# Turning the state-space values by VectorE and DRAM instead of TensorE, in a two-layer hybrid decoder on one core

## The chip, the core and the metric

One core of a Trainium2 chip runs the whole program in one launch. The metric is the device time of a launch in microseconds (us). Engines are named as in the profile: PE is TensorE's matmul row, PEld its weight load, DVE is VectorE, ACT is ScalarE, POOL is GpSimd, SP is the engine that issues most DMAs; a q behind a name (SPq, POOLq) is the engine's sequencer. L285 is line 285 of the kernel before.

## The reference

Two layers work on a sequence of 512 positions of width 1024, in float32. Each layer is

```python
hn = rmsnorm(x, pre_g)
proj = hn @ w_in                      # 1024 -> 6664, split into thirteen parts
y = concat([retention(q, k, v) * silu(g),            # 4 heads of 128, chunks of 128
            ssd_mixer(xbc, z, dt, ...),              # 8 heads of 64, 2 groups, state 128
            stick_breaking(q, k, v) * silu(g),       # 4 heads of 128
            memory_read(q, mem_n, w_mem_kv) * silu(g)])  # 4 heads of 128, 256 memory tokens
x = x + rmsnorm(y @ w_out, post_g)
```

The part that the change touches is the state-space mixer (`ssd_mixer`). In it a convolution and a SiLU give `xs` (values), `bm` and `cm`; then

```python
xdt = x_heads * delta[..., None]                     # values times step size
y_diag = einsum('bclsgj,bcsgjp->bclgjp', cb[..., None] * decay_in, xdt)
states = einsum('bclgn,bclgjp->bcgjpn', bc, xdt * decay_states[..., None])
y = rmsnorm_by_group((y_diag + y_off + x_heads * d_skip) * silu(z))
```

## The kernel before, in words

Activations lie features first: a tile of 128 features by 512 positions. Projections run as three fp32r products (high by high, high by low, low by high) of a split weight and a split activation; that is `mm3`, and nearly all of TensorE's time.

**Weights.** Both layers' weights come in 78 blocks of up to 1 MB, two subs of 128 x 1024 to a block, 156 subs in all (`k` = 0 to 155; 78 to a layer). `w_prefetch` splits a sub: ScalarE copies it to the high part, VectorE subtracts for the low part (`split`, L293 and L294). Five subs have a buffer (`NSUB = 5`), so sub `k` can be split when `k - 5` has been used. In the first half of the output projection and in the per-head projections a sub lasts 24 matmuls of 512 columns; in the second half of the output projection the four banks run two steps apart (`SKEW = 2`), so four subs are in use at once.

**Order.** `tick()` counts units, one to a projection of 128 columns (two to some others). `defer(n, f)` writes the work of `f` into the program `n` units later. A planner then fixes each engine's instruction order from the program order and its own estimate of what is ready; `keep_in_program_order` pins an instruction behind everything already written for its engine. Every engine runs its list strictly in order, and so does the SP queue that issues nearly all small DMAs.

**State-space group** (`ssd_group`, twice a layer). Units: the two value tiles `X["x"]`, a stick-breaking gate, B, C, a gate, two z gates. `ssd_values`, two units after the values, turns the two tiles of 128 features by 512 positions on TensorE (eight transposes of 128 x 128 into PSUM, L1003), multiplies by `delta` into `xdt` (L1007) and by the decay into `xds` (L1009). `ssd_mix`, `ssd_states` and `ssd_out` follow with their matmuls, then `ssd_var` (sum of squares, a one-row product, the row through ScalarE, DRAM and GpSimd to a broadcast) and `ssd_norm` (L1075), whose results the output projection uses as its last four inputs (`kc` 12 to 15).

**Turning through DRAM** (`columns_turned`) exists already for B and for retention's keys: VectorE transposes 32 x 32 blocks (L660), four DMAs per tile write the blocks to their places in DRAM (L663), and a read brings the turned tile back (L668).

**Retention** (`ret_head`, ..., `ret_head3`). `ret_head3` makes the one-row product of two heads and sends it the same way (ScalarE L808, SP L811, GpSimd L812 and L813, SP L815 and L818); `scaled` (L886) multiplies it in, seven units later.

**Tile pools**: 33 tiles "s", 16 "y", 9 "r" of 128 x 512; PSUM four banks "pj" (projections) and four "mx".

Of the kernel before, what the change touches and what calls it, by code (L numbers as in the profile page):

```python
# [8 lines left out]
F32 = mybir.dt.float32  # L9
# [3 lines left out]
ALU = mybir.AluOpType  # L13
# [3 lines left out]
P = 128  # L17
# [52 lines left out]
NBLK = len(BLOCKS)  # L70
# [4 lines left out]
def block_width(b):  # L75
    return 2 * (SUBD if BLOCKS[b % NBLK][0] == "d" else SUBW)
# [77 lines left out]

BLK = 32
TT = "y"
ST, SL, SB1, SB2 = "s", "y", 2, 4
ROW = 128  # L160

# [9 lines left out]
def v3(ap, a):  # L171
    return ap.rearrange("p (a b) -> p a b", a=a)


class Builder:
# [136 lines left out]
    def w_prefetch(self, upto=None, between=()):  # L312
        if self.starting and upto is None:
            return
        while self.w_split < (upto or min(self.nsubs, self.w_cur + self.NSUB)):
            k = self.w_split
            self.w_load(k // 2)
            n = block_width(k // 2) // 2
            h, l = (self.wp.tile([P, SUBW], F32R, tag=t, name=self.name(t), bufs=self.NSUB)[:, :n] for t in ("wh", "wl"))
            r = self.raw[k // 2]  # L320
            if isinstance(r, list):
                pieces = [(r[2 * (k % 2) + i][:], slice(512 * i, 512 * i + 512)) for i in range(2)]
            else:
                cs = [slice(0, n)] if k > 1 else [slice(0, n // 2), slice(n // 2, n)]
                pieces = [(r[:, (k % 2) * n + c.start:(k % 2) * n + c.stop], c) for c in cs]
            for i, (x, c) in enumerate(pieces):
                self.split(x, h[:, c], l[:, c], h[:, c].bitcast(F32))
                if i < len(between):
                    between[i]()
            self.sub[k] = (h, l)  # L330
            self.w_split += 1
            if k % 2:
                del self.raw[k // 2]
                if not self.starting:
                    self.w_load(k // 2 + self.NRAW)

    def w_load(self, b):
        while self.w_dma <= min(b, DEPTH * NBLK - 1):
            n = block_width(self.w_dma)
            src = self.a["wts"][self.w_off:self.w_off + P * n].rearrange("(p n) -> p n", p=P)  # L340
            if self.starting and self.w_dma == 2:
                r = [self.new(512, F32, "y") for _ in range(4)]
                for i in range(4):
                    self.nc.sync.dma_start(r[i][:], src[:, 512 * i:512 * i + 512])
            else:
                r = self.wp.tile([P, 2 * SUBW], F32, tag="raw", name=self.name("raw"), bufs=self.NRAW)
                if self.starting:
                    for c in ((slice(0, n),) if self.w_dma > 1 else (slice(0, n // 2), slice(n // 2, n))):
                        self.nc.sync.dma_start(r[:, c], src[:, c])  # L349
                        if not self.w_dma and not c.start:  # L350
                            self.mem_start()
                else:
                    self.nc.scalar.dma_start(r[:, :n], src)
            self.raw[self.w_dma] = r
            self.w_dma += 1
            self.w_off += P * n
# [273 lines left out]
    def mem_turn(self, h, w, y):  # L630
        nc = self.nc
        pT = []
        for m in range(2):
            T = self.buf(tag="y")
            for i in range(2):
                x = w[i].rearrange("p (t m j b) -> p m t j b", t=2, m=2, b=BLK)[:, m]
                nc.vector.transpose(T.rearrange("p (j t b) -> p t j b", t=NT, b=BLK)[:, 2 * i:2 * i + 2], x)
            d = self.turned_rows(P, SEQ)
            dd = d.rearrange("(j m) (a t) -> a m j t", m=BLK, a=P // BLK)
            pT.append(self.through_dram(T, dd, d, self.buf(tag="y")))  # L640
# [5 lines left out]
    def through_dram(self, T, dst, src, out):  # L646

        n = dst.shape[2]
        for a in range(P // BLK):
            self.nc.sync.dma_start(dst[a], v3(T[BLK * a:BLK * a + BLK], n))  # L650
        self.nc.sync.dma_start(out, src)
        return out

    def columns_turned(self, tiles, out):
# [3 lines left out]
        for k, x in enumerate(tiles):  # L658
            T = self.buf(n, TT)
            self.nc.vector.transpose(T, x)  # L660
            dd = d[:, P * k:P * k + P].rearrange("(b t) (a f) -> a t b f", t=BLK, a=P // BLK)
            for a in range(P // BLK):
# [188 lines left out]
    def ret_head2(self, h, v, sc, f, st, q, y):  # L851

        nc = self.nc
        b, o = self.mx(), slice(HD * h, HD * h + HD)
        for i in range(2):
            c = slice(2 * P * i, 2 * P * i + 2 * P)
            p = v[2 * i][0]
            self.mm3(b[:, c], p.h[:, o], p.l[:, o], sc.h[:, c], sc.l[:, c], True, False)
            if i:
                self.mm3(b[:, c], st[:, :P], st[:, P:], q.h[:, c], q.l[:, c], False, False)  # L860
            self.mm(b[:, 2 * P * i + P:2 * P * i + 2 * P], v[2 * i + 1][1][:, o], f[:, P * i:P * i + P], False, True)
        nc.scalar.copy(y, b)
        sq = self.buf(tag="r")
        nc.scalar.activation(sq, b, AF.Square, scale=HD ** -0.5)
        for n in (64, 32):
            nc.vector.tensor_add(sq[0:n], sq[0:n], sq[n:2 * n])
        if h % 2 == 0:
            self.z = self.new(512, F32R, "r"), []
        z, ys = self.z
        r = 64 * (h % 2)  # L870
        nc.scalar.copy(z[r:r + 32], sq[0:32])
        nc.vector.tensor_sub(z[r + 32:r + 64], sq[0:32], z[r:r + 32].bitcast(F32))
        ys.append(y)
        if h % 2:
            self.defer(3, self.ret_head3, h // 2, z, ys)

    def ret_head3(self, i, z, ys):

# [80 lines left out]
    def ssd_group(self, l, g, ysb):  # L959

        X = {"l": l, "g": g}
        self.ssd_decay(X)
        X["x"] = [self.conv(self.proj_b(), 2 * g + i) for i in range(2)]
        self.defer(2, self.ssd_values, X)
        self.gated(("sb", 2 * g), ysb[2 * g])
        X["b"] = self.conv(self.proj_b(), 4 + g)
        X["bt"] = self.buf()[:, :3 * P]
        self.columns_turned([X["b"][:, :3 * P]], [X["bt"]])
        X["c"] = self.conv(self.proj_b(), 6 + g)
        self.defer(3, self.ssd_mix, X)  # L970
        self.gated(("sb", 2 * g + 1), ysb[2 * g + 1])
        X["y"] = [self.buf(tag="y"), self.buf(tag="y")]
        X["z"] = [self.gate(self.proj_b()) for _ in range(2)]
        self.defer(1, self.ssd_states, X)
        self.defer(3, self.ssd_out, X, 0)
        self.defer(3, self.ssd_out, X, 1)
        self.defer(5, self.ssd_var, X)
        self.defer(9, self.ssd_norm, X)

    def ssd_decay(self, X):  # L980
        nc, S = self.nc, self.ssd
# [12 lines left out]
    def ssd_values(self, X):  # L994

        nc, g = self.nc, X["g"]
        X["xdt"], X["xds"] = [], []
        for i in range(2):
            b = self.mx()
            for c in (2 * i, 2 * i + 1):  # L1000
                for j in range(2):
                    o = 256 * (c % 2) + P * j
                    nc.tensor.transpose(b[:, o:o + P], X["x"][j][:, P * c:P * c + P], self.con("ident", P))  # L1003
            xdt, xds = self.buf(), self.buf()
            for c in (2 * i, 2 * i + 1):
                s = slice(256 * (c % 2), 256 * (c % 2) + 256)
                nc.vector.tensor_tensor(out=v3(xdt[:, s], 4), in0=v3(b[:, s], 4), in1=self.per_head("delta", g, c), op=ALU.mult)  # L1007
                if c < NT - 1:
                    nc.vector.tensor_tensor(out=v3(xds[:, s], 4), in0=v3(xdt[:, s], 4), in1=self.per_head("dst", g, c), op=ALU.mult)  # L1009
            X["xdt"].append(xdt)  # L1010
            X["xds"].append(xds)
# [323 lines left out]
```

## Time and profile before

| | |
|---|---|
| runs | 922.54, 922.68, 923.47 us; median 922.68 |
| the profiled execution | 923.25 us, of it 921.5 us from the first to the last instruction |
| busy: PE / DVE / ACT / POOL | 913.2 / 673.3 / 443.5 / 146.3 us |
| instructions: PE / DVE / ACT / POOL | 4667 / 1081 / 841 / 208 |
| DMA | 128.53 MB; mean 139 GB/s over the span |

Matmuls overlap in a pipeline, so what a matmul costs is the distance from its start to the next start and not its own duration; the view of the chain that ended last gives those distances, summed over stretches.

### The profile page before, as it was taken

The numbers are of one execution on the slowest core, as the hardware profiler recorded it, in microseconds if no ns is written. First come the engines' busy times: TensorE is split into PE (matmuls) and PEld (weight loads), VectorE is DVE, ScalarE is ACT, GpSimd is POOL, SyncE is SP. The second block draws the span as 40 slices with busy tenths as digits, with TensorE's granted clock in tenths as the row PEclk, the third lists the DMA queues.
The fourth block names the chain that finished last, engine by engine and source line by source line (L and its number), as shares of the span: only waits on it lengthen the run. The fifth ranks groups of instructions, "written<-read, shape, count | busy, mean of one in ns | idle before, by whom it ended". The sixth has DMA issues, their size and how long they took to land.

```text
span 921.5 us, 12952 instructions
## 1 busy us (share of the span) xinstructions
PE 913.2 (99%) x4667; PEld 773.6 (84%) x4667; DVE 673.3 (73%) x1081; ACT 443.5 (48%) x841; POOL 146.3 (16%) x208
## 2 busy tenths in 40 slices
PE   9999999999999999999999999999999999999997
PEld 7998888888888888888899888888888888888885
DVE  6855689888787887844587476898778869687343
ACT  6643485744453342733465336675445434335341
POOL 1200152320131110100040002423112120102001
PEclk9999999999999999999999999999999999999999
DMA  8544664642444333444345256556333362422502
GB/s 316 213 141 144 169 167 104 199 146 61 120 134 148 116 109 126 137 149 158 116 173 196 93 172 183 124 122 183 103 109 116 110 194 92 139 95 88 210 12 91
DMA packets 105408, 128.53 MB, mean 139 GB/s; under 512 B 64640, under 2 KB 79744, under 8 KB 96256
## 3 DMA queue, kind: packets, MB, share of 16 engines
q10 hardware_dynamic: 10224, 73.44, 23.4%
q1 hardware_dynamic: 95120, 54.28, 20.7%
q8 instruction: 36, 0.59, 0.3%
q14 instruction: 28, 0.23, 0.1%
HBM read 112.10 MB, written 15.56 MB: 139 GB/s over the span
## 4 chain that ended last, share of the span: by engine, by line
PE 98%; DMA 1%; ACT 0%; DVEq 0%; SPq 0%; POOLq 0%; issue 0%; POOL 0%; ACTq 0%; DVE 0%
PE pj L285 74%; PE mx L285 23%; PE mx L479 1%; DMA mem<-memT 1%; PE mx L1003 0%; ACT s L523 0%; DVEq L1331 0%; ACT s L1168 0%; POOLq L1331 0%; ACT wh L293 0%; SPq L506 0%; SPq L349 0%; SPq L1206 0%; POOL t L449 0%; ACTq L1331 0%
## 5 line engine op out<-in xcount | busy, mean ns | idle before, releaser
L285 PE MATMUL pj<-hTh,wh 128*128 128x512 f32 x704 | 276.4, 393 | 0.0
L285 PE MATMUL pj<-hTh,wl 128*128 128x512 f32 x704 | 275.8, 392 | 0.0
L285 PE MATMUL pj<-hTl,wh 128*128 128x512 f32 x704 | 274.6, 390 | 0.0
L294 DVE TENSOR_TENSOR wl<-raw,wh 128x1024 fp32r<-128x1024 f32 (+2 forms) x156 | 188.6, 1214 | 116.9 <-ACT wh L293 115.7
L293 ACT CAST wh<-raw 128x1024 fp32r<-128x1024 f32 (+2 forms) x156 | 158.7, 1020 | 205.0 <-PE pj L285 177.5
L285 PEld LDWEIGHTS pj<-hTh,wl 128*128 128x128 f32 x704 | 132.2, 188 | 27.3
L285 PEld LDWEIGHTS pj<-hTh,wh 128*128 128x128 f32 x704 | 132.3, 188 | 27.1 <-DVE s L593 0.8
L285 PEld LDWEIGHTS pj<-hTl,wh 128*128 128x128 f32 x704 | 132.3, 188 | 26.6
L285 PE MATMUL pj<-wh,s 128*128 128x512 f32 x320 | 97.6, 391 | 0.0
L285 PE MATMUL mx<-s,s 128*128 128x256 f32 (+4 forms) x528 | 79.7, 307 | 0.0
L285 PE MATMUL mx<-wh,s 128*128 128x512 f32 x256 | 79.2, 389 | 0.0
L285 PEld LDWEIGHTS mx<-s,s 128*128 128x128 f32 (+1 forms) x528 | 65.8, 177 | 8.2 <-PE pj L285 1.4
L285 PEld LDWEIGHTS pj<-wh,s 128*128 128x128 f32 x320 | 59.7, 188 | 12.4
L285 PE MATMUL pj<-wl,s 128*128 128x512 f32 x160 | 60.2, 389 | 0.0
L285 PEld LDWEIGHTS mx<-wh,s 128*128 128x128 f32 x256 | 48.1, 188 | 10.0
L294 DVE TENSOR_TENSOR s<-y,s 128x512 fp32r<-128x512 f32 x64 | 41.2, 687 | 19.7 <-ACT s L293 14.0
L262 ACT ACTIVATE s<-s 128x128 f32<-128x128 f32 (+3 forms) x96 | 41.8, 478 | 22.3 <-DVE s L733 20.6
L675 POOL TENSOR_TENSOR s<-y,s 128x512 fp32r<-128x512 f32 x16 | 23.7, 1494 | 179.9 <-ACT s L674 179.4
L293 ACT CAST s<-y 128x512 fp32r<-128x512 f32 x64 | 36.6, 617 | 30.8 <-PE mx L285 22.0
L285 PE MATMUL mx<-wl,s 128*128 128x512 f32 x128 | 49.6, 389 | 0.0
L285 PE MATMUL pj<-wl,hTh 128*128 128x256 f32 (+2 forms) x144 | 47.6, 331 | 0.0
L285 PE MATMUL pj<-wh,hTl 128*128 128x256 f32 (+2 forms) x144 | 47.5, 330 | 0.0
(185 smaller groups left out, 1298.5 us busy)
## 6 DMA issues: line engine op xcount, KB each, us to landing
raw<-wts ACTq DMA_DIRECT2D x69, 1024.0 KB, 4.8
s<-x SPq DMA_DIRECT2D x24, 256.0 KB, 4.1
y<-turned SPq DMA_DIRECT2D x24, 256.0 KB, 2.8
turned<-y SPq DMA_DIRECT2D x64, 64.0 KB, 2.2
s<-acs SPq DMA_DIRECT2D x16, 256.0 KB, 6.3
r<-row SPq DMA_DIRECT2D x12, 256.0 KB, 5.0
raw<-wts SPq DMA_DIRECT2D x4, 512.0 KB, 7.5
raw<-wts SPq DMA_DIRECT2D x2, 1024.0 KB, 6.3
```

Of the source, the lines that this page charges most:

```text
L262: i = self.nc.scalar.activation(out, in_, func, **k)
L285: return self.nc.tensor.matmul(out, lhsT, rhs, start=start, stop=stop)
L293: self.nc.scalar.copy(h, src)
L294: self.nc.vector.tensor_sub(l, src, hf)
L479: x = self.nc.tensor.transpose(b[:, P * j:P * j + P], hn[i][:, P * j:P * j + P], self.con("ident", P))
L675: nc.gpsimd.tensor_sub(p.l, x, p.hf)
```

## The change

1. The value tiles are turned by `columns_turned` right after their convolution, into two "r" tiles; the 32 TensorE transposes (8 to a group, 2 groups, 2 layers) are gone. `xdt` is written over the turned tile. `ssd_values` comes four units after the values instead of two, and the first multiplication by `delta` of each tile is pinned in program order.
2. `ret_head3` comes five units after its second head instead of three.
3. `ssd_var` and `ssd_norm` come two units later (7 and 11 for 5 and 9).
4. The low part of every third sub (`k % 3 == 2`, from 14 on, without those with `k % 78` from 16 to 33) is subtracted by GpSimd instead of VectorE: 36 of 156 subs.

```diff
+VD, HOLD = 4, True
 BLK = 32
-TT = "y"
+TT, TX = "y", "r"
...
-                self.split(x, h[:, c], l[:, c], h[:, c].bitcast(F32))
+                nc = self.nc
+                nc.scalar.copy(h[:, c], x)
+                (nc.gpsimd if self.low_by_pool(k) else nc.vector).tensor_sub(l[:, c], x, h[:, c].bitcast(F32))
...
+    def low_by_pool(self, k):
+
+        return k > 12 and k % 3 == 2 and not 16 <= k % (2 * NBLK) < 34
...
-            self.defer(3, self.ret_head3, h // 2, z, ys)
+            self.defer(5, self.ret_head3, h // 2, z, ys)
...
-        self.defer(2, self.ssd_values, X)
+        X["xt"] = [self.buf(tag=TX), self.buf(tag=TX)]
+        self.columns_turned(X["x"], X["xt"])
+        self.defer(VD, self.ssd_values, X)
...
-        self.defer(5, self.ssd_var, X)
-        self.defer(9, self.ssd_norm, X)
+        self.defer(7, self.ssd_var, X)
+        self.defer(11, self.ssd_norm, X)
...
-            b = self.mx()
-            for c in (2 * i, 2 * i + 1):
-                for j in range(2):
-                    o = 256 * (c % 2) + P * j
-                    nc.tensor.transpose(b[:, o:o + P], X["x"][j][:, P * c:P * c + P], self.con("ident", P))
-            xdt, xds = self.buf(), self.buf()
+            b = xdt = X["xt"][i]
+            xds = self.buf()
             for c in (2 * i, 2 * i + 1):
                 s = slice(256 * (c % 2), 256 * (c % 2) + 256)
-                nc.vector.tensor_tensor(out=v3(xdt[:, s], 4), in0=v3(b[:, s], 4), in1=self.per_head("delta", g, c), op=ALU.mult)
+                k = nc.vector.tensor_tensor(out=v3(xdt[:, s], 4), in0=v3(b[:, s], 4), in1=self.per_head("delta", g, c), op=ALU.mult)
+                if HOLD and not c % 2:
+                    self.tc.keep_in_program_order(k)
```

## Rows read from the trace of the kernel before

**Rows 1.** The head of the page: the span, the busy time of each engine (share of the span, instructions), and the granted TensorE clock in 40 equal slices (9 is 90% or more).

```profile
span 921.5 us, 12952 instructions
PE 913.2 (99%) x4667; PEld 773.6 (84%) x4667; DVE 673.3 (73%) x1081; ACT 443.5 (48%) x841; POOL 146.3 (16%) x208
PEclk9999999999999999999999999999999999999999
```

**Rows 2.** All waits of the PE in the whole span: who waited for whom, us in total, times, the longest.

```profile
PE mx L285 <- POOL b L197: 1.2, 1, 1.2
PE pj L285 <- ACT s L523: 1.0, 2, 0.7
```

**Rows 3.** The transposes' own line: count, duration in ns (minimum, median, maximum), first and last start.

```profile
L1003 PE MATMUL mx<-consts,s x32: 270/272/273, 268.5 to 775.4; 128*128 128x128 f32 x32
```

**Rows 4.** Timeline of the PE around the last six transposes of the first layer: start, length, engine, line and operation.

```profile
322.31 0.82 PE L1003 MATMUL mx<-consts,s 128*128 128x128 f32 x6
322.88 0.48 PE L285 MATMUL pj<-hTh,wh 128*128 128x512 f32 x1
323.19 0.40 PE L285 MATMUL pj<-hTl,wh 128*128 128x512 f32 x1
```

**Rows 5.** The chain that ended last, 255 to 345 us (the state-space groups of the first layer): start, us that the chain spent there, engine, line, count.

```profile
268.63 0.22 PE mx L1003 x2
...
272.75 0.11 PE mx L1003
...
273.20 0.55 PE mx L1003 x5
...
285.34 13.61 PE pj L285 x60
298.96 2.19 PE mx L285 x14
...
319.47 0.22 PE mx L1003 x2
319.69 2.78 PE pj L285 x12
322.47 0.66 PE mx L1003 x6
323.12 15.47 PE pj L285 x68
```

**Rows 6.** The same view of the second layer, 707 to 798 us: two of its five groups of transposes (x2, x1, x5, x2, x6 again).

```profile
725.73 0.55 PE mx L1003 x5
...
774.99 0.66 PE mx L1003 x6
```

**Rows 7.** Timeline of the way that B takes through DRAM in the first group: the transpose of three quarters of a tile, four writes, one read (for the SP queue the length is that of the issues).

```profile
283.34 0.58 DVE L660 STREAM_TRANSPOSE y<-s 128x384 f32<-128x384 f32 x1
283.94 1.86 SPq L663 DMA_DIRECT2D turned<-y  x4
289.05 0.39 SPq L668 DMA_DIRECT2D s<-turned  x1
```

**Rows 8.** By line: all VectorE transposes of the kernel (ns), and, of L663 between 255 and 345 us, the time from issue to landing.

```profile
L660 DVE STREAM_TRANSPOSE y<-s x12: 431/446/579, 195.0 to 787.5; 128x256 f32<-128x256 f32 x8, 128x384 f32<-128x384 f32 x4
...
DMA to landing us min/median/max: 2.8/3.5/4.2
```

**Rows 9.** By line or tile: the low part of a tile of 128 x 512 on GpSimd (ns), and the low part of a weight sub on VectorE.

```profile
L675 POOL TENSOR_TENSOR s<-y,s x16: 1285/1298/2285, 108.6 to 587.9; 128x512 fp32r<-128x512 f32 x16
L294 DVE TENSOR_TENSOR wl<-raw,wh x156: 681/1225/1809, 5.3 to 897.9; 128x1024 fp32r<-128x1024 f32 x144, 128x528 fp32r<-128x528 f32 x8, 128x512 fp32r<-128x512 f32 x4
```

**Rows 10.** The last weight sub (`k` = 155) in the timelines of ACT and DVE, and the chain's row of the second half of the last output projection.

```profile
896.78 1.04 ACT L293 CAST wh<-raw 128x1024 fp32r<-128x1024 f32 x1
...
897.86 1.23 DVE L294 TENSOR_TENSOR wl<-raw,wh 128x1024 fp32r<-128x1024 f32 x1 [0.26 <-ACT wh L293]
...
871.96 43.53 PE mx L285 x192
```

**Rows 11.** Timelines between the layers: GpSimd's part of the norm of the second block of positions, the normed rows on VectorE, their turning on the PE.

```profile
470.40 1.55 POOL L444 TENSOR_SCALAR t<-t 128x1 f32<-128x1 f32 x1 [2.38 <-ACT s L462]
...
472.31 0.57 POOL L450 TENSOR_TENSOR t<-t,mhalf 128x1 f32<-128x1 f32 x1
...
472.91 1.42 DVE L470 SCALAR_TENSOR_TENSOR s<-s,t,s 128x512 f32<-128x512 f32 x2 [0.44 <-POOL t L450]
...
477.04 0.60 PE L479 MATMUL mx<-consts,s 128*128 128x128 f32 x4
```

**Rows 12.** Timelines in the first state-space group: the end of the second value tile's convolution, two of the multiplications by `delta`, ScalarE's copy of retention's row, the end of C's convolution.

```profile
269.43 0.69 DVE L943 SCALAR_TENSOR_TENSOR s<-s,s 128x512 f32<-128x512 f32 x1 [0.76 <-ACT s L267]
...
273.46 0.76 DVE L1007 TENSOR_TENSOR s<-mx,t 128x256 f32<-128x256 f32 x2 [0.37 <-PE mx L1003]
...
285.38 0.58 ACT L808 COPY r<-mx 2x512 f32<-2x512 f32 x1 [3.17 <-PE mx L285]
...
293.75 0.68 DVE L943 SCALAR_TENSOR_TENSOR s<-s,s 128x512 f32<-128x512 f32 x1
```

**Rows 13.** Timelines of the norm of the last state-space group in the second layer: the one-row product, and the two normed tiles.

```profile
831.43 0.40 PE L285 MATMUL mx<-r,onesr 128*1 128x512 f32 x1
...
846.60 1.41 DVE L1075 SCALAR_TENSOR_TENSOR y<-y,consts,r 128x512 f32<-128x512 f32 x2 [4.92 <-DMA r<-row]
```

## The prediction, made before the changed kernel ran

> **What bounds the kernel now.** I read the page's head first, then the PE's waits, then the chain that ended last. The head shows the PE busy for 913.2 of 921.5 us, at the full clock (2.4 GHz) in every slice [rows 1]. Busy alone could hide short stalls, so the waits decide: in the whole span the PE waited 2.2 us, all of it at the start [rows 2]. The chain runs along the PE from first to last matmul. So the time is the sum of the distances between matmul starts, and nothing else counts unless it makes the PE wait. Every other engine works under cover, and the question for each edit is whether it shortens the PE's list or uses up cover.
>
> **What leaves the PE.** 32 transposes. A transpose lasts 272 ns [rows 3], but behind six in a row that start at 322.31 the next matmul starts at 322.88 and the one after at 323.19 [rows 4]: 0.88 us for six transposes and a matmul. The chain counts distances: 0.22 + 0.11 + 0.55 + 0.22 + 0.66 = 1.76 us for the 16 of a layer [rows 5], 110 ns each; the second layer repeats it [rows 6]. Both: 3.52 us. A second, smaller term: behind a group of transposes the projection's matmuls are further apart for a while. The twelve at 319.69 take 2.78 us, 232 ns each, where sixty undisturbed ones take 13.61, 227 each [rows 5]: 0.06 us. The 68 behind the group of six take 15.47, 0.04 over that pace. With two or three such places a layer this is 0.1 to 0.3 us in all. Sum: 3.5 to 3.8, I take 3.6 us.
>
> The Trainium skill (TensorE: Matmul & The Clock Gate, Part 4: PE-mode transpose) gives about 275 ns for a transpose inside a kernel. The trace's duration agrees, but its starts lie 110 ns apart; by the page's figure the sum would be an estimated 8.8 us, by the rows it is 3.52.
>
> **What the values cost on their new way.** Per tile one VectorE transpose of 512 columns: 446 ns for 256 and 578 for 384 [rows 7, 8], so 710 estimated; eight of them, 5.7 us of VectorE. The multiplications stay, with the same shapes. Per group eight writes and two reads on SP: the writes take 0.47 us each to issue (1.86 for four), the read 0.39 [rows 7], 4.5 us of SP per group. Landing: two transposes start when the second value tile is done (269.43 + 0.69 = 270.1 [rows 12]) and end at 271.5; the last write is issued near 275 and lands 2.8 to 4.2 us later [rows 8], at 278 to 279.5; two reads and their landing, at B's scale (B's whole way took 8.1 us), put the turned tiles at 282 to 284. If retention's row DMAs, which wait for GpSimd, stand ahead of them in SP's list, add up to 5 us: 289.
>
> When are they wanted? The pinned multiplication stands behind C's convolution, which ended at 294.4 [rows 12]. That convolution had been held up by ScalarE, which waited 3.17 us for retention's row product with its list standing behind; that product now comes two units (10.9 us) later, so C's convolution may end as early as 286. So the tiles land before or about when VectorE turns to them. The first PE reader is `ssd_states`, in the fourteen matmuls at 298.96 (eight of `ssd_mix` first) [rows 5], then `ssd_out`. Seven multiplications at 0.38 us (two in 0.76 [rows 12]) after 286 to 289 end by 292: some 7 us of cover for the PE. I price this edit at nothing on the PE. If the cover went, VectorE would stand at the pinned instruction, with gates, convolutions and weight low parts queued behind it, and the PE would stop for `ssd_states`.
>
> **Retention's row and the state-space norm.** Moving `ret_head3` moves one product, one ScalarE copy, two GpSimd steps and five DMAs past the group's decay loads on SP; `scaled` moves with it, and its first reader is the retention gate, two units and more behind. No PE cost. The norm is closer. In the second layer its row product ran at 831.43 and the normed tiles were ready at 846.60 + 1.41 = 848.0 [rows 13], 16.6 us later. Two units move it to about 842.3 and 858.9; splitting them for the PE needs about 2 us more: 861. The second half of that projection starts at 915.50 - 43.53 - 0.17 = 871.8 [rows 10], and `kc` 14 is first used 24 matmuls of 0.227 before that, at 866.4. Cover about 5 us. Price nothing, bounded by a GpSimd low part ahead of it in the list.
>
> **Low parts on GpSimd.** VectorE gives up 34 subtractions of 1.225 us and two of 0.7: 43 us. On GpSimd half the columns took 1.285 to 2.285 us [rows 9], so a sub takes 2.6 (quiet) to 4.6 us (VectorE busy beside it), 1.3 to 3.4 more than now. In the per-head stages a sub is split four subs ahead of its use, 4 x 24 x 0.227 = 21.8 us: cover enough. Two places are tight. (a) The last sub, `k` = 155: its high part ends at 897.82, so GpSimd ends at 900.4 to 902.4. It is first used at step 14 of the skewed order, behind 132 matmuls: 871.8 + 132 x 0.2267 = 901.7 [rows 10]. Nothing, to 0.7 us of stall; VectorE, idle for 0.26 us before it, would have nothing else there, so I take nothing. (b) Between the layers GpSimd also makes the norms. A norm step began at 470.40 after 2.38 us of idle time, into which a low part of 2.6 to 4.6 us fits but for 0.2 to 2.2 us; the normed rows, ready at 472.91 + 1.42 = 474.33, would be later by that, and the PE turns them at 477.04 [rows 11]: 2.7 us of cover. I take nothing here too.
>
> **The sum.** The profiled execution took 923.25 us (span 921.5 and 1.75 around it), 0.57 above the median of the runs. 923.25 - 3.6 = 919.65; by the median, 922.68 - 3.6 = **919.1 us**.
>
> **The rivals.**
>
> *B: a low part comes late.* GpSimd's subtraction takes the long figure at (a), or the norms of two or three position blocks slip past their cover at (b). For: GpSimd's spread of 1.285 to 2.285 lies where VectorE is busy. Against: cover of 1.3 and 2.7 us. It decides from 3.9 us per sub at (a). Price 0.7 to 2.4 us: 919.8 to 921.5.
>
> *C: the values come late, slower than before.* Place: the pinned multiplication, four times. It costs the PE only where the tiles land after about 296, twelve us behind my estimate; from 0.9 us of PE stall a group on the gain is gone. At 2 to 4 us a group: 919.1 + 8 to 16 = 927 to 935. For: ten DMAs more on one in-order SP queue, in which any waiting DMA holds the rest, and turned tiles, retention's rows and its centred values share nine "r" tiles. Against: B's way took 8.1 us with half as many writes. The Trainium skill (VectorE: DVE Perf Modes, The three transpose paths) warns that a strided plain copy used as a transpose is 19 times slower than the DMA's transposing path; with its 1309 ns that is an estimated 25 us, which would bring C about. By that rule the writes crawl; in the trace they land in 2.8 to 4.2 us [rows 8].
>
> *D: no change.* The planner, with new ready times, cuts small matmuls into more pieces or lets the PE wait briefly at several readers. The first matmul of a returning projection takes 0.31 us [rows 4] where others take 0.227, so pieces at some 0.1 us alone give back under 1 us; short waits of about 1 us at three of the four groups give back the rest: about 922.5.
>
> *E: transposes cost their duration.* 32 x 0.272 = 8.7 us gone: 914.0. Rows 4 and 5 speak plainly against it.
>
> **How the numbers follow.** Forecast 0.68, B 0.10, C 0.10, D 0.10, E 0.02. Measurements of this kernel tell about 0.2%, 1.85 us, from no change: faster is below 920.8, slower above 924.5. Faster: 0.68 + 0.07 of B + 0.02 = 0.77; same: 0.03 of B + 0.10 = 0.13; slower 0.10. The forecast's own range is 918.5 to 919.9 (gain 3.5 to 3.8, spread of the runs). The range reaches over B and half of D: 918.3 to 922.2; outside lie E, C and the rest of D, under 0.2.
>
> **What would show it.** Right: 4635 PE instructions, no line of transposes in the state-space groups, PE waits still about 2 us and all at the start, DVE near 673 - 43 + 6 = 636 us, POOL up by 90 to 160 us. Wrong: a PE wait for "s" or "r" tiles of `ssd_states` or `ssd_out`, or DVE idle for a DMA into "r" near 285 (C); a PE wait for a GpSimd-written "wl" near 900 or for "hTh" near 477 (B); several waits under 2 us in the groups (D).

## The result, and the profile after

The changed kernel took 925.52 us (median of 7 runs, 924.7 to 927.58) against 923.16 (922.54 to 923.58) for the kernel before on the same chip: a ratio of 1.0029, interval 1.0019 to 1.0038. It is slower by 0.3%, where 0.4% faster was forecast. The profiled execution took 926.32 us. The head of its page answers [rows 1]:

```profile
span 924.6 us, 12980 instructions
...
PE 911.6 (99%) x4635; PEld 770.4 (83%) x4635; DVE 670.3 (72%) x1053; ACT 441.7 (48%) x841; POOL 231.2 (25%) x244
...
PEclk9999999999999999999999999999999999999999
```

The 32 transposes are gone (4667 to 4635 PE instructions) and the clock is full. Yet the distance from the first to the last matmul start grew from 913.86 to 916.88 us. All waits of the PE answer [rows 2] (who waited for whom, us in total, times, the longest):

```profile
PE pj L286 <- ACT s L530: 1.9, 2, 1.6
PE mx L286 <- DVE s L950: 1.7, 2, 0.9
PE mx L286 <- POOL b L198: 1.2, 1, 1.2
PE mx L286 <- DVE r L879: 1.0, 2, 0.6
PE mx L286 <- DVE s L1040: 1.0, 2, 0.6
```

The first and third stand at the start, as before (the first differs from execution to execution). The three "twice" rows on VectorE are new, once in each layer's first state-space group. The timeline of the PE shows two of the three places of the first layer (start, length, engine, line, operation, the idle time and what ended it):

```profile
291.08 0.39 PE L286 MATMUL pj<-hTh,wl 128*128 128x512 f32 x1
292.04 0.39 PE L286 MATMUL mx<-r,onesr 128*2 128x512 f32 x1 [0.57 <-DVE r L879]
...
295.67 0.39 PE L286 MATMUL pj<-hTh,wh 128*128 128x512 f32 x1
296.95 0.82 PE L286 MATMUL mx<-s,s 128*128 128x128 f32 x5 [0.89 <-DVE s L950]
```

Matmuls that start 0.227 us apart stand 0.96 and 1.28 apart here, a third pair (at 313.77) 0.68. The second layer repeats it at 744.69, 749.20 and 767.26 (0.84, 1.24, 0.89). Over 0.227 each, the six make some 4.5 us; the start took 0.9 more than in the profile before; 3.5 were saved. That leaves 1.9 of the 3.0 us explained, and 1.1 spread too thinly to be placed.

What VectorE did in front of these places, by its timeline. Line numbers are those of the kernel that was run: in the changed kernel L1012 is the multiplication by `delta`, L1016 that by the decay, L950 the end of a convolution, L879 a step of retention's row, L1040 the sum of the states.

```profile
282.56 0.56 DVE L667 STREAM_TRANSPOSE y<-s 128x384 f32<-128x384 f32 x1
288.30 0.43 DVE L1012 TENSOR_TENSOR r<-r,t 128x256 f32<-128x256 f32 x1 [5.17 <-DMA r<-turned]
...
291.21 0.69 DVE L879 TENSOR_TENSOR r<-r,r 32x512 fp32r<-32x512 f32 x1
292.11 1.54 DVE L947 SCALAR_TENSOR_TENSOR s<-pj,hp,s 128x511 f32<-128x511 f32 x2 [0.21 <-ACT s L945]
...
295.69 0.42 DVE L1012 TENSOR_TENSOR r<-r,t 128x256 f32<-128x256 f32 x1
296.20 0.69 DVE L950 SCALAR_TENSOR_TENSOR s<-s,s 128x512 f32<-128x512 f32 x1
296.81 0.42 DVE L1012 TENSOR_TENSOR r<-r,t 128x256 f32<-128x256 f32 x1
297.26 2.60 DVE L1016 TENSOR_TENSOR s<-r,t 128x256 f32<-128x256 f32 x1
```

VectorE stood 5.17 us at a multiplication by `delta`, waiting for the turned tile, while retention's row (L879, behind pieces left out here) and C's convolution (L947, L950) stood behind it: these are the two that the PE then waited for. The diff holds chunks 0 and 2 alone (`not c % 2`). The multiplication at 288.30 is one that isn't held: with all four held, none stands there (below). By the program's order it is chunk 1; the trace doesn't number the buffers. The planner had put it directly behind B's transpose. Three of the four (288.30, 290.76, 295.69) stand ahead of the end of C's convolution, L950, though two alone are unheld; only the one at 296.81 stands where I had expected them all. So a pin doesn't always put an instruction behind everything written before it, as the words on the kernel have it.

And why the tile was late, by the timelines of ACT's and SP's queues, with the time from issue to landing by line:

```profile
275.45 0.33 ACTq L360 DMA_DIRECT2D raw<-wts  x1
...
276.29 0.50 SPq L822 DMA_DIRECT2D row<-t  x1
276.84 0.58 SPq L670 DMA_DIRECT2D turned<-y  x1
280.81 1.29 SPq L825 DMA_DIRECT2D r<-row  x2
282.15 0.43 SPq L670 DMA_DIRECT2D turned<-y  x1
285.38 0.88 SPq L675 DMA_DIRECT2D r<-turned  x2
```

```profile
L360 ACTq DMA_DIRECT2D raw<-wts x1: 334/334/334, 275.4 to 275.4; - x1
...
DMA to landing us min/median/max: 5.2/5.2/5.2
...
L822 SPq DMA_DIRECT2D row<-t x1: 499/499/499, 276.3 to 276.3; - x1
...
DMA to landing us min/median/max: 4.5/4.5/4.5
```

SP's list has retention's row between the writes of the second value tile: L822 waited for GpSimd's pow (272.89 + 3.38, done at 276.3), L825 for the row's landing. That row is 4 KB, but it was issued 0.8 us behind a weight transfer of 1 MB and landed with it, at 280.8. So the last write went out at 282.15 and the tile was there at 288.2, in my upper case of 289.

GpSimd's low parts and what they cost VectorE, by line:

```profile
L330 POOL TENSOR_TENSOR wl<-raw,wh x36: 1527/2396/2872, 48.9 to 900.9; 128x1024 fp32r<-128x1024 f32 x34, 128x528 fp32r<-128x528 f32 x2
...
L330 DVE TENSOR_TENSOR wl<-raw,wh 128x1024 fp32r<-128x1024 f32 (+2 forms) x120 | 146.6, 1226 | 84.7 <-ACT wh L329 73.1 <-issue 10.5 <-DVE r L873 0.4
```

VectorE's own low parts fell from 188.6 to 146.6 us, but its busy time only from 673.3 to 670.3: the eight new transposes brought 5.6 us, and other instructions became longer (the L1016 above, 2.60 us instead of 0.42, ran beside a GpSimd subtraction).

### The profile page after: what moved, and what is told of

It is laid out like the page before. It is cut to its first block, busy times and chain, and to the rows that moved or that the text cites. A ratio compares the mean times of both kernels' runs of the same rounds, so it can differ in the third digit from the quotient of the medians.

```text
span 924.6 us, 12980 instructions
## 1 busy us (share of the span) xinstructions
PE 911.6 (99%) x4635; PEld 770.4 (83%) x4635; DVE 670.3 (72%) x1053; ACT 441.7 (48%) x841; POOL 231.2 (25%) x244
## 4 chain that ended last, share of the span: by engine, by line
PE 91%; DVE 3%; DMA 3%; ACT 1%; issue 1%; POOL 0%; SPq 0%; DVEq 0%; POOLq 0%; ACTq 0%
PE pj L286 69%; PE mx L286 22%; DVE wl L330 1%; PE mx L486 1%; DMA mem<-memT 1%; DMA s<-acs 1%; DMA row<-t 0%; POOL t L820 0%; DVE y L893 0%; DMA turned<-y 0%; ACT wh L329 0%; DVE s L1016 0%; DMA r<-turned 0%; DVE s L997 0%; DVE s L1027 0%
## 5 line engine op out<-in xcount | busy, mean ns | idle before, releaser
L330 DVE TENSOR_TENSOR wl<-raw,wh 128x1024 fp32r<-128x1024 f32 (+2 forms) x120 | 146.6, 1226 | 84.7 <-ACT wh L329 73.1
L330 POOL TENSOR_TENSOR wl<-raw,wh 128x1024 fp32r<-128x1024 f32 (+1 forms) x36 | 86.3, 2396 | 266.1 <-ACT wh L329 224.0
L286 PE MATMUL mx<-s,s 128*128 128x256 f32 (+3 forms) x400 | 72.8, 317 | 2.8 <-DVE s L950 1.7
L286 PEld LDWEIGHTS mx<-s,s 128*128 128x128 f32 x400 | 59.1, 189 | 10.8 <-DVE s L950 2.6
L295 DVE TENSOR_TENSOR s<-y,s 128x512 fp32r<-128x512 f32 x64 | 49.0, 809 | 20.2 <-ACT s L294 14.4
```

The lines of the kernel that those rows point to most:

```text
L286: return self.nc.tensor.matmul(out, lhsT, rhs, start=start, stop=stop)
L295: self.nc.vector.tensor_sub(l, src, hf)
L330: (nc.gpsimd if self.low_by_pool(k) else nc.vector).tensor_sub(l[:, c], x, h[:, c].bitcast(F32))
```

## The experiments

### What the transposes were worth

The kernel before with its 32 transposes left out; the multiplications take the values unturned:

```
-  nc.tensor.transpose(b[:, o:o + P], X["x"][j][...], ident)
```

> The kernel before with the 32 transposes of the values left out: the multiplications read the unturned tiles, so the state-space values are not the reference's; nothing else differs. This is the price of the transposes by itself. Expected from the chain of the kernel before: 3.5 to 3.8 us faster than before, ratio 0.9960. If transposes cost their own 272 ns: 8.7 us.

919.46 us against 922.99, ratio 0.9964 (0.9951 to 0.9977): 3.5 us. The first term of the sum was right, and the rival that counted durations falls.

### The multiplications that were not held

All four held:

```
-  if HOLD and not c % 2:
+  if HOLD:
```

> All four multiplications by delta of a group are pinned in program order, not the first and third alone. Theory (the free second multiplication was placed ahead of C's convolution and VectorE stood there 5.2 us for its tile, which made the PE wait some 2.3 us in each layer's first group): the wait of VectorE for the turned tile goes from 11.8 us to under 2, the PE's waits in the groups go, and the time falls by 4 to 5 us from the changed kernel, to 920.5 to 921.5. Rival (GpSimd's low parts hold up VectorE, whatever the pins): the waits at the third place stay and the time falls by under 1.5 us, to 924 or more.

920.71 us, ratio 0.9978 (0.9968 to 0.9988), 4.8 us below the changed kernel. VectorE in the same place, and the landing of the same reads, issued at 283.80 and 284.21:

```profile
288.83 0.69 DVE L950 SCALAR_TENSOR_TENSOR s<-s,s 128x512 f32<-128x512 f32 x1 [0.76 <-ACT s L268]
289.54 0.43 DVE L1012 TENSOR_TENSOR r<-r,t 128x256 f32<-128x256 f32 x1
...
290.79 2.64 DVE L1016 TENSOR_TENSOR s<-r,t 128x256 f32<-128x256 f32 x1
```

```profile
L675 SPq DMA_DIRECT2D r<-turned x2: 371/420/469, 283.8 to 284.2; - x2
...
DMA to landing us min/median/max: 5.7/5.9/6.0
```

The tile landed at 289.51, 1.3 us later than in the changed kernel, and VectorE waited for nothing: C's convolution ended at 289.52 instead of 296.89. So it is not the lateness but the place in VectorE's list that decided, with luck in the size: a tile that lands later still would be waited for here too. The PE had no stall in the first layer's groups; one of 3.4 us in the second layer (760.82) came after VectorE had stood 4.18 us for a decay row (756.58), below.

None held:

```
-VD, HOLD = 4, True
+VD, HOLD = 4, False
```

> The changed kernel with none of the four multiplications held. VectorE's list then has all four ahead of C's convolution, the first at the place where the changed kernel's first unheld one stands. Theory (the loss comes from the first unheld multiplication, whatever the held ones do): the wait at 288 stays at 5 to 6 us and the time is 924.5 to 926.5, as changed. Rival (the held ones, which stand late, delay the values' users): 921 to 923.5.

931.51 us, ratio 1.0092 (1.0079 to 1.0105). The wait at 285.94 is 5.48 us, as the theory said, but the time is 5 us above its range: beside the waits of the changed kernel for L879 and L950 the PE waited 4.2 us for L1040 (1.0 there), and its clock fell to 0.80 for 311 to 316 us. The held half had been worth 6 us.

Retention's product back at three units:

```
-  self.defer(5, self.ret_head3, h // 2, z, ys)
+  self.defer(3, self.ret_head3, h // 2, z, ys)
```

> The changed kernel with retention's row product back at three units after its pair of heads (before: three, changed: five); everything else as changed, and the lists of VectorE and of SP around the values keep the same order. Theory (the loss is VectorE standing at an unheld multiplication by delta for the turned tile): that wait stays at 4.5 to 6 us in the first group of each layer and the time is 924.5 to 926.5. Rival (the move of the row product is what costs: the stall of 1 us at 291 is its product waiting for VectorE's L879): that stall goes, and the time is 922 to 923.5.

925.69 us, ratio 1.0027 (1.0017 to 1.0037); VectorE's waits 5.09 and 5.14 us. As the theory said, the move is worth nothing. What changes is which reader the PE meets first: it now waits 4.6 us, all for L879.

The rows' write and reads issued by GpSimd, so that SP doesn't stand between the writes:

```
-  nc.sync.dma_start(d.rearrange(...), c)
+  nc.gpsimd.dma_start(d.rearrange(...), c)
...
-  nc.sync.dma_start(out[i], d[i:i + 1].to_broadcast([P, SEQ]))
+  nc.gpsimd.dma_start(out[i], d[i:i + 1].to_broadcast([P, SEQ]))
```

> The changed kernel, where the write and the broadcast reads of every 1/rms row are issued by GpSimd, right behind the pow that they need, instead of by SP, where they stand between the writes of the turned values. Theory (the tile is late because SP stands in its list, first for the pow and then for the row's landing): the second tile's last write is issued by 277 to 278 instead of 282, the tile lands by 280 to 283 instead of 288.2, VectorE's wait for it falls from 5.2 us to under 2.5, and the time is 920.5 to 922.5, although the multiplications are held as in the changed kernel. Rival (the landing is late because the transfers themselves are slow then): it lands after 286, the wait stays over 4 us, and the time is 924 to 926.5.

926.88 us, ratio 1.0031 (1.0016 to 1.0046). Half right: the last write went out at 274.64 instead of 282.15 and the tile landed at 283.5 and 285.8, but VectorE still waited 2.94 and 1.30 us, and the time didn't fall. The writes of 274.1 landed at 280.1, again with the weights; and the planner, which now took the tile for early, put the multiplications even ahead of B's transpose, so that the PE waited 0.8 us for turned B and more in the second groups. A late tile is not cured by sending it earlier when the planner moves its readers forward as well.

### The low parts

The changed kernel with all low parts on VectorE:

```
-  (nc.gpsimd if self.low_by_pool(k) else nc.vector).tensor_sub(...)
+  nc.vector.tensor_sub(...)
```

> The changed kernel with all weight low parts on VectorE again, pins as changed. Theory: VectorE still stands 5 us for the turned tile twice; the time falls by 0 to 1.5 us (the 2.6 us that a multiplication took beside a low part on GpSimd is gone), to 924 to 925.5. Rival (the low parts are the cause): 3 to 5 us faster than the changed kernel, 920.5 to 922.5.

920.94 us, ratio 0.9976 (0.9967 to 0.9985). My theory (924 to 925.5) was wrong, its rival right. The multiplications stand where they did in the changed kernel, but the tile was there earlier:

```profile
270.37 0.50 SPq L822 DMA_DIRECT2D row<-t  x1
...
272.13 0.93 SPq L825 DMA_DIRECT2D r<-row  x2
...
279.26 0.99 SPq L675 DMA_DIRECT2D r<-turned  x2
```

```profile
282.04 0.43 DVE L1012 TENSOR_TENSOR r<-r,t 128x256 f32<-128x256 f32 x1 [1.99 <-DMA r<-turned]
```

Here the planner had retention's row ahead of the first tile's writes. L822 left at 270.37 instead of 276.29, ahead of the next weight transfer (271.82) and not behind one, and landed in 1.7 us instead of 4.5. VectorE waited 2 us instead of 5 in the first group; in the second groups it waited longer than in the changed kernel (2.96 and 3.48 us for 0.54 and 0.82), so that in sum it stood nearly as long for turned tiles (10.6 us for 11.8), and the PE's waits in the groups come to 0.4 us. This run takes away the late tile of the first groups and the low parts on GpSimd at once. Which of the two gave the 4.6 us it doesn't separate; holding alone was enough, with the low parts left on GpSimd.

The low parts alone, on the kernel before:

```
-  self.split(x, h[:, c], l[:, c], h[:, c].bitcast(F32))
+  nc.scalar.copy(h[:, c], x)
+  (nc.gpsimd if self.low_by_pool(k) else nc.vector).tensor_sub(...)
```

> The kernel before with only the low parts on GpSimd that the change put there (36 subtractions of 128x1024); values, retention and norm as before. Theory (the low parts price nothing by themselves: they are done in time, and what they stretch on VectorE has cover): 922.3 to 923.7, like before. Rival 1 (VectorE instructions beside them are stretched to 2.3 to 2.6 us, and that reaches TensorE): 924 or more. Rival 2 (VectorE's freed time shortens its waits): 920 to 922.

925.27 us, ratio 1.0025 (1.0015 to 1.0035): 2.1 us slower, the first rival. VectorE and GpSimd in the first state-space group:

```profile
271.81 0.69 DVE L949 SCALAR_TENSOR_TENSOR s<-s,s 128x512 f32<-128x512 f32 x1 [0.76 <-ACT s L267]
...
293.10 2.46 DVE L949 SCALAR_TENSOR_TENSOR s<-s,s 128x512 f32<-128x512 f32 x1 [2.19 <-ACT s L267]
295.48 1.27 DVE L957 SCALAR_TENSOR_TENSOR s<-s,pj 128x512 f32<-128x512 f32 x2
296.68 1.69 DVE L1088 SCALAR_TENSOR_TENSOR y<-y,s 128x512 f32<-128x512 f32 x1
```

```profile
292.48 2.92 POOL L819 TENSOR_TENSOR t<-t,mhalf 64x16 f32<-64x16 f32 x1
295.38 2.44 POOL L329 TENSOR_TENSOR wl<-raw,wh 128x1024 fp32r<-128x1024 f32 x1
```

The end of C's convolution took 2.46 us instead of 0.68 [rows 12] and ended 0.2 us behind the start of the low part, which GpSimd began as soon as its pow was done. The pow by itself didn't do it: the same L949 at 271.81 ran beside a pow too (271.36 to 274.27), with no low part directly behind that one, and took 0.69. L1088 started beside the low part and ended 0.6 behind it, at 298.37. The two L957 between them, which read a projection in PSUM, took 0.67 each and were not held. VectorE's busy time is 663.8 us, 9.5 below the 673.3 before, although some 42 us of subtractions left it: some 33 came back as longer instructions.

Where does that reach the PE? The same with 28 of the 36, without the eight in the first groups, and with these eight alone:

```
+  ... and not 47 <= k % (2 * NBLK) < 59     # 28 low parts
+  ... and 47 <= k % (2 * NBLK) < 59         # the other eight
```

> The kernel before with 28 of the 36 low parts on GpSimd: the eight that fall into the first state-space group of a layer (at 257, 277, 295 and 314 us and their like in layer 2) stay on VectorE. Theory B (stretched instructions in that group): the time is 922.3 to 923.7, like before. Rival C (the stretch, or what else the low parts do, costs everywhere): 924.5 to 926.

> The kernel before with only those eight low parts on GpSimd. Theory B: they carry the whole cost, 924.3 to 926. Rival C: 922.3 to 923.7.

923.89 us for the 28, ratio 1.0006 (0.9997 to 1.0015), 0.2 above the theory's range and no change within the noise; 925.90 for the eight, 1.0031 (1.0020 to 1.0042). The eight carry all that is measured. Waits of the PE with the 28:

```profile
PE mx L285 <- POOL b L197: 1.2, 1, 1.2
PE pj L285 <- ACT s L529: 1.1, 2, 0.8
```

and with the eight:

```profile
PE mx L285 <- DVE s L1039: 2.3, 2, 1.4
...
```

Elsewhere the longer instructions cost the PE nothing; in these groups `ssd_out` waits for the state sum (L1039) at the end of VectorE's work.

The other explanation, decay rows that land late behind a row's write:

```
-  nc.sync.dma_start(v3(a, 4), S["rows"][0, r:r + 4]...)
+  nc.gpsimd.dma_start(v3(a, 4), S["rows"][0, r:r + 4]...)
```

> The kernel before with the 36 low parts on GpSimd (925.27 us), and the decay rows read by transfers that GpSimd issues. Theory A (the 2 us are the decay rows, late behind a row's write on SP): the stall of 1.5 us at 311 goes and the time is 922.3 to 923.5. Theory B (they are VectorE's instructions stretched beside GpSimd's): little changes, 924.5 to 926.

928.72 us, ratio 1.0047 (1.0033 to 1.0061). The stall at 311 stayed (1.47 us; 1.50 where SP issued the reads), so that explanation falls; that it became slower still, by stalls of 1.0 and 2.0 us in the second layer, neither had said.

### The next wait

All held and no low parts on GpSimd, two remedies at once:

> All four multiplications pinned, and all weight low parts on VectorE as before. Theory: same as with the pins alone within 0.7 us, 920 to 921.5, since VectorE has room for the 43 us. Rival (GpSimd's low parts cost): 1 to 2 us faster than with the pins alone.

934.23 us, ratio 1.0122 (1.0109 to 1.0135), against theory and rival: both together should have gained. VectorE in the second group, then the PE, then the stretch from 355 to 359 us (busy time of PE, PEld, DVE, ACT, POOL, then the PE's clock, DMA share, GB/s):

```profile
345.32 0.42 DVE L1012 TENSOR_TENSOR r<-r,t 128x256 f32<-128x256 f32 x1
352.84 1.42 DVE L1082 SCALAR_TENSOR_TENSOR y<-y,consts,r 128x512 f32<-128x512 f32 x2 [7.10 <-DMA r<-row]
354.17 0.42 DVE L1016 TENSOR_TENSOR s<-r,t 128x256 f32<-128x256 f32 x1
```

```profile
354.73 0.67 PE L286 MATMUL mx<-s,s 128*128 128x256 f32 x2 [3.57 <-DVE s L1016]
```

```profile
355.00:359.00 4.00, 4.00 (x13) 3.19 (x12) 4.00 (x7) 0.00 (x0) 0.00 (x0) 0.63 0.01 2
```

The same fault with another instruction. The norm of the first group (L1082), not held, was put between the held multiplications, and VectorE stood 7.1 us for its row. The PE stood 3.6 us for L1016, and behind that its matmuls came 0.43 us apart instead of 0.227 and the granted clock over 355 to 359 us was 0.63: part of that stretch ran at the lower of the two clock levels (1.2 GHz). With the norm held as well:

```
+  self.tc.keep_in_program_order(
       self.nc.vector.scalar_tensor_tensor(out=y, ..., in1=X["rB"], ...))
```

> The kernel of the second run (all four multiplications held, every low part on VectorE, 934.23 us) with one thing more: the two products of the state-space norm are held in program order too. Theory (its 13 us are VectorE standing 7.1 us at the norm's product, which the planner put between the held multiplications and which waits for a broadcast): those waits go, the products of the second group are not held up, and the time is 919 to 921.5. Rival (VectorE with all low parts and held multiplications is too full): 931 to 935.

923.43 us, ratio 1.0003 (0.9993 to 1.0013): 11 us came back, between the two expectations. What was left are VectorE's waits of 4.2 and 3.9 us for decay rows (L997) in the first groups. Their reads stand in SP's list behind L822, which waits for GpSimd's pow. Without that:

> The kernel with all low parts on VectorE, four multiplications and the norm held (923.43 us), and again the decay rows read by transfers that GpSimd issues. Theory: what was left there was VectorE's 4.2 and 3.9 us for decay rows in the first groups, with TensorE stalls of 1.5 and 2.6 us and half clock behind the second; these go, and the time is 919.2 to 921. Rival (VectorE is too full without GpSimd's help, so other waits take their place): 922.5 to 924.

919.93 us, ratio 0.9963 (0.9951 to 0.9975), and no PE wait but those at the start: as the theory said for the time. But VectorE still waited 3.6 us at one L997 in each layer, which the PE didn't see, so that these waits were what had cost the 3.5 us is not shown.

### A version that beats both

All held, low parts on GpSimd as changed, and the rows or the decay rows issued by GpSimd:

> Both remedies at once: all four multiplications held, and the rows' writes and reads issued by GpSimd. Theory: the two remedies meet at the same wait, so together they give hardly more than either: 919.3 to 921.3, with under 1 us of TensorE stalls in a layer's first group; the waits of VectorE for the decay rows (s<-acs, 4.2 us at 756.58 in the first run) get shorter too, since those reads stood behind a row's write on SP. Rival (transfers issued by GpSimd land later or hold up its low parts): 922 to 926.

> The kernel of the first run (all four multiplications held, 920.71 us), where the decay rows (s<-acs) are read by transfers that GpSimd issues, so that they no longer stand in SP's list behind a row's write that waits for GpSimd's pow. Theory (the 3.4 us stall of layer 2 in that run's profile was VectorE standing 4.2 us for a decay row): VectorE's wait for decay rows in the first groups falls under 1.5 us, no stall over 1 us is left there, and the time is 919.2 to 920.4. Rival (transfers that GpSimd issues hold up its own list, as the rows did): 921 to 923.

With the rows: 922.47 us, ratio 0.9988 (0.9979 to 0.9997), in the rival's range and 1.8 us more than with held multiplications alone, though its profile has only 0.6 us of new PE waits; why is open. With the decay rows: 919.34 us, ratio 0.9963 (0.9951 to 0.9976), as the theory said, 6 us below the changed kernel. Its PE waits:

```profile
PE pj L286 <- ACT s L530: 1.5, 2, 1.2
PE mx L286 <- POOL b L198: 1.3, 1, 1.3
PE pj L286 <- ACT wh L329: 0.9, 1, 0.9
```

None is in a state-space group, and the 3.5 us that the transposes were worth are all there. The last run took the eight low parts back to VectorE:

> The kernel of the eleventh run (all held, decay rows by GpSimd, 919.34 us) with those eight low parts back on VectorE. Theory: no TensorE stall is left in those groups, so there is nothing to gain: 918.8 to 920.2. Rival (the stretched instructions still cost there): 917 to 918.5.

926.98 us, ratio 1.0042 (1.0028 to 1.0055), against both. VectorE behind the first group's `ssd_out`:

```profile
330.03 0.55 DVE L1061 TENSOR_TENSOR s<-s,mx 128x384 f32<-128x384 f32 x1 [5.39 <-DMA s<-acs]
```

Once more an instruction that is not held, once more a transfer; the PE waited 2.9 us for L1074 in the two layers. The row's read was issued at 322.61, 0.07 us behind a weight transfer, and took 7.40 us to land; in the run of 919.34 us the same read left at 323.32 with no weight transfer under way and took 2.80. The second layer repeats it (0.26 us behind one, 5.39 for 3.05). So the price of a low part here hangs on what its move does to the order and the timing of the rest.

## Why the prediction was wrong, point by point

- **The bound: right as far as the losses could be placed.** They are PE waits or their aftermath in the clock; 1.1 us of the changed kernel and 1.8 us of the run with the rows by GpSimd were not placed.
- **The transposes, 3.5 to 3.8 us: right**, 3.5 measured.
- **The values, priced at nothing: the step that failed.** "The pinned multiplication stands behind C's convolution" holds for one of four. Two are not held, and one of these stood directly behind B's transpose, where VectorE came free at 283.1 and waited until 288.3 with C's convolution and retention's row behind it. The landing was within my bounds (288.2 of 282 to 289), but the cover of 7 us was counted for a multiplication behind the convolution. Holding all four brought 4.8.
- **Rival C** had the mechanism (VectorE at a multiplication, gates and convolutions behind it), and its condition, a landing after 296, was wrong for the same reason: the price began at 283. Two places instead of four, some 2.3 us each.
- **Retention's row, nothing: right in the sum** (925.52 with the move, 925.69 without). The norm's move was not tried by itself; the version of 919.34 us has it and no PE wait in a group. That retention's DMAs may stand ahead on SP was the upper bound, and came about.
- **Low parts, nothing: wrong, by 2.1 us.** This is the second step that failed, measured on the kernel before. I expected GpSimd to take 2.6 to 4.6 us beside a busy VectorE; it took 2.40 nearly every time, and VectorE's instructions took the waiting. So VectorE came to 670 us instead of 636. I looked for the price where a low part is late (rival B: the last sub, between the layers), where none showed; it lay in the first state-space group, where the PE waits for the end of VectorE's work. It is no constant: with all held and the decay rows by GpSimd, all 36 stayed on GpSimd and the full gain was there.
- **The sum** held the two edits apart. In the changed kernel they met: each remedy alone, holding or no GpSimd, took back 4.8 and 4.6 us, so their prices can't be added.

## What to carry to other kernels

On an engine with an in-order list, an instruction that waits for a transfer holds all that stands behind it: before pricing a moved value by when it is wanted, look up where each copy of its reader really stands, and hold every one of them behind the work that needs no transfer. Then look for the next such reader, since a remedy changes the order and may expose it. Work moved to a helper engine was free only where what it made longer on the main engine had slack.

## What the runs showed of the hardware

**GpSimd's low parts held VectorE, its small pows didn't.** In the eighteen traces (before, changed, sixteen experiments) 212 VectorE instructions with both inputs in SBUF started beside a GpSimd low part of 128 x 1024, and every one ended 0.28 to 1.09 us behind it: 0.42 us became 2.60 (L1016). None of the 260 with an operand in PSUM became longer. The Trainium skill (SBUF — State Buffer, SBUF: two separate sides) says that a GpSimd instruction and a VectorE one with two SBUF inputs exclude each other for a whole instruction, whichever starts first; for the low parts the traces agree, with GpSimd first and VectorE as the loser in these rows. I had not weighed that rule. For the pows of 64 x 16 and 32 x 16, some 3 us each, the traces differ from it: 279 such VectorE instructions started beside one that had no GpSimd instruction of 512 or more columns directly behind it, and all kept their length; of 68 beside one that had, 11 became longer.

**A small transfer issued behind a weight transfer landed with it.** In the changed kernel 4 KB took 4.5 us to land when issued 0.8 us behind a weight transfer of 1 MB (5.2 us). In the eighteen traces 25 such rows were issued 0.5 to 1 us behind one and took 4.76 us (median, 4.04 to 6.71), landing 0.17 us (median) behind the weights; 51 with none under way or just behind took 1.67 (median).
